# Layer 2's differential attention: a tile's transposes directly behind the next tile's scores, with the filling matmuls after them

## The chip, the cores and the metric

The kernel runs on one core of a Trainium2 chip. The metric is the time of one execution in device microseconds. A core has TensorE (matmuls and transposes into PSUM banks), VectorE, ScalarE, GpSimd and the DMA queues; the engines run side by side and wait for each other through semaphores. In the profile PE is TensorE's matmuls, PEld its weight loads, DVE is VectorE, ACT ScalarE, POOL GpSimd, SP the queue that issues most loads.

## The reference

A two-layer backbone with 512 latent tokens, 256 context tokens, a width of 1024. Each layer has a mixer of four branches (Fourier, convolution, grouped-query attention, differential attention), gated and merged, and then a SwiGLU part. In the second layer only the 512 latent tokens are updated, and they read all 768. The branch that the change touches:

```python
def diff_attend(q, k, v, lam):
    s = jnp.einsum("bhmqd,bhmkd->bhmqk", q, k).astype(jnp.float32) * (DIFF_QK_DIM ** -0.5)
    p = jax.nn.softmax(s, axis=-1)
    w = (p[:, :, 0] - lam * p[:, :, 1]).astype(v.dtype)
    return jnp.einsum("bhqk,bhkd->bhqd", w, v)
```

There are four heads; each has two score maps (m = 0 and 1), and a root-mean-square norm follows on each head's output.

## The kernel before, in words

All large matmuls are done on operands split into a high and a low part, three matmuls for one product (L607 to L609 in the filling units). The differential attention runs through `steps`, four heads by four tiles of 128 queries in layer 2 (`last` is true, `nqt` is 4). For a tile:

- `issue(i)` puts the tile's scores on TensorE (L904, eight matmuls into the one PSUM buffer `pS`) and the negated row maximum on VectorE (L910, L912).
- `exps` makes the two exponentials on ScalarE (L923), which read `pS`.
- `combine` makes the weights of the difference in place in `es[0]` on VectorE (L1379, L1380, L1382).
- `transp` transposes that tile on TensorE (L933, six transposes into two PSUM banks of the tag T, named `pT`), copies them on ScalarE as the high part (L935) and subtracts for the low part on VectorE (L936).
- In every second tile (p odd) 18 matmuls multiply by the values (L1432), two transposes spread the sums (L1437), and L1442 and L1443 write the output.

The work is in a stretch of manual schedule: TensorE, VectorE and ScalarE take instructions in the order in which the program issues them. Between these parts the program issues filling: `fill.run(w)` first pumps side work, then issues chunks of gate units (six matmuls of 512 columns each, some 1.4 us), as far as its budget reaches. In layer 2 the budget of a step is 3.84 us of matmuls, shared out by `DF = (0.55, 0.15, 0.3, 0.0)` over four places in the step. A gate unit has four chunks of a gate's projection, a tanh on ScalarE (L779), two chunks of the branch's product, and VectorE's merge (L786, L787). After each chunk `stream.feed` keeps the weights coming: loads (L557 on SP's queue), the cast of the high part on ScalarE (L563), the low part on VectorE (L570).

Side work is a list of generators, each with the matmul time (`clk`) before which it isn't resumed. `pump` resumes those that are due:

```python
for e in list(self.side):
    if e[1] <= clk[0]:
        next(e[0])
        e[1] = clk[0] + gap
```

Two of them use T banks on TensorE: `od_norm`, the norm of a head's output, parked at the end of its head and resumed in the next (L1218 square, L1226 sums into a bank, L167 and L169, L1234 transposes into a bank, L1235), and `conv_ln`, the convolution's layer norm, in head 0 (L948, L951, L955 mean into a bank, L957 to L963, later L970 and L977). The tag T has two banks:

```python
def bank():
    return pp.tile([P, 512], F32, tag="T", name="pT", bufs=2)
```

The last tile's step of a head (`end`) makes the next head's keys, queries and values in place of the filling.

Of the kernel before, what the change touches and what calls it, by code (L numbers as in the profile page):

```python
# [62 lines left out]
def block_kernel(ctx: ExitStack, tc: tile.TileContext, x, c, ctx_in, c_ctx, w_ada, b_ada, norm_mix, w_in,  # L63
# [148 lines left out]
    def drain(g):  # L212
        for _ in g:
            pass
# [36 lines left out]
    def bank():  # L251
        return pp.tile([P, 512], F32, tag="T", name="pT", bufs=2)
# [366 lines left out]
    for l in range(DEPTH):  # L619
        last = l == DEPTH - 1  # L620
# [5 lines left out]
        GF, DF = GF_[l], DF_[l]  # L626
# [3 lines left out]
        with ExitStack() if l else first as st:  # L630
# [27 lines left out]
            def pttile():  # L658
                t = sp.tile([P, 2, 6, 2 * P], F32R, tag="pt", name="pt", bufs=1)
                return t, t.rearrange("p w k (i q) -> p w k i q", i=2)  # L660
# [43 lines left out]
            def run_taps(n, free=False):  # L704
                with ExitStack() if free else tc.issue_after(lastv[0]):
                    for _ in range(min(n, len(tapq))):
                        tapq.pop(0)()
# [186 lines left out]
            def scores(q, k, ks, t, ko, nk):  # L894
                S = sbank()
                for a in range(2):
                    cuts = [0, 512, NTOK] if a == 0 else [0, 256, NTOK]
                    for c0, c1 in zip(cuts, cuts[1:]):
                        c1 = min(c1, nk)
                        if c0 >= c1:  # L900
                            continue
                        for i in range(2):
                            clk[0] += (c1 - c0) / 2400.0
                            nc.tensor.matmul(S[:, a, c0:c1], lhsT=q[:, a, t * P:(t + 1) * P],  # L904
                                             rhs=k[i][:, ks[a], ko + c0:ko + c1], start=(i == 0), stop=(i == 1))
                return S

            def row_max(S, nk, scale):
                nm = smp.tile([P, 2], F32, tag="nm", name="nm")
                nc.vector.reduce_max(nm, S[:, :, :nk], axis=AX.X, negate=True)  # L910
                if isinstance(scale, float):
                    nc.vector.tensor_scalar(nm, nm, scale, None, op0=ALU.mult)  # L912
                else:
                    nc.vector.tensor_mul(nm, nm, scale)
                return S, nk, scale, nm

            def exps(S, nk, scale, nm):
                ss = smp.tile([P, 2], F32, tag="ss", name="ss")
                es = []
                for a in range(2):  # L920
                    e = etile(nk, "e")
                    sc = scale if isinstance(scale, float) else scale[:, a:a + 1]
                    nc.scalar.activation(e, S[:, a, :nk], AF.Exp, bias=nm[:, a:a + 1], scale=sc, accum_out=ss[:, a:a + 1])  # L923
                    es.append(e)
                return es, ss

            def transp(e, pt, i, nkt):
                clk[0] += nkt * 0.107
                for a in range(0, nkt, 4):
                    b = min(nkt, a + 4)  # L930
                    pb = bank()
                    for t in range(a, b):
                        nc.tensor.transpose(pb[:, (t - a) * P:(t - a + 1) * P], e[:, t * P:(t + 1) * P], ident)  # L933
                    src = pb[:, :(b - a) * P].rearrange("p (t q) -> p t q", q=P)
                    nc.scalar.copy(pt[:, 0, a:b, i], src)  # L935
                    nc.vector.tensor_sub(pt[:, 1, a:b, i], src, pt[:, 0, a:b, i])  # L936

            def krange(t):
                return (0, NTOK) if t < 4 else (X, CT)
# [52 lines left out]
            def conv_split(i0, i1):  # L992
                rr = [(0, X, 0)] if last else [(0, X, 0), (X, NTOK, CO)]
                for i in range(i0, i1):
                    y = stile([2, NTOK], F32R, "yc")
                    for a, b, o in rr:
                        v = ca[i][:, o:o + b - a]
                        nc.scalar.copy(y[:, 0, a:b], v)
                        nc.vector.tensor_sub(y[:, 1, a:b], v, y[:, 0, a:b])
                    yc.append(y)  # L1000

            def ytile(name):
                return sp.tile([P, NT], F32, tag="y", name=name, bufs=4 if last else 2)
# [170 lines left out]
            def wt(t):  # L1174
                return 1.0 if t < 4 else 0.45
# [75 lines left out]
            with tc.manual_schedule(engines=ENG):  # L1251
# [5 lines left out]
                fill = Filler()  # L1257
# [20 lines left out]
                def issue(i):  # L1278
                    j, t = steps[i]
                    ko, nk = krange(t)  # L1280
                    S = scores(qbox[j], qbox["k"], (j // 2, j // 2), t, ko, nk)
                    rq = qs[j][1]
                    return row_max(S, nk, rq[:, 2 * t:2 * t + 2])
# [111 lines left out]
                for i, (hd, t) in enumerate(steps):  # L1395
                    p = i % nqt
                    if cln is None and not tapq:
                        cln = conv_ln()
                        fill.park(cln, 0.0)
                    if hd == 3 and p == nqt - 1:  # L1400
                        drain(cln)
                        conv_split(0, 3)
                    if p == 0:
                        o = ytile("yd")
                        yd.append(o)
                        v = box["v"]
                    ko, nk = krange(t)
                    k0, nkt_ = ko // P, nk // P
                    end = p == nqt - 1
                    if not end:  # L1410
                        nm_ = issue(i + 1)
                        fill.run(wt(t) * DF[0])
                    elif hd < 3:
                        fill.rest()
                        fill.take()
                    if p % 2 == 0:
                        pt, pt5 = pttile()
                    transp(w_, pt5, p % 2, nkt_)
                    if not end:
                        es = exps(*nm_)  # L1420
                        fill.run(wt(t) * DF[1])
                    elif hd < 3:
                        fill.take()
                        dv = fill.take(True)
                    else:
                        fill.rest()
                    if p % 2 == 0:
                        pvs = pp.tile([P, 512], F32, tag="pv", name="pv", bufs=1)
                    if p % 2 == 1:
                        for i_, (vi, pi) in enumerate(((0, 0), (1, 0), (0, 1))):  # L1430
                            for kt in range(nkt_):
                                nc.tensor.matmul(pvs[:, :256], lhsT=v[:, vi, k0 + kt], rhs=pt[:, pi, kt],  # L1432
                                                 start=(kt == 0 and i_ == 0), stop=(kt == nkt_ - 1 and i_ == 2))
                        clk[0] += nkt_ * 0.32
                        lo = (t - 1) * P
                        for u_ in range(2):
                            nc.tensor.transpose(pvs[:, 256 + u_ * P:256 + (u_ + 1) * P],  # L1437
                                                rss[p - 1 + u_][:, 0:1].to_broadcast([P, P]), ident)
                    if not end:
                        fill.run(wt(t) * DF[2])  # L1440
                    if p % 2 == 1:
                        nc.scalar.copy(o[:, lo:lo + 256], pvs[:, :256])  # L1442
                        nc.vector.tensor_mul(o[:, lo:lo + 256], o[:, lo:lo + 256], pvs[:, 256:])  # L1443
                    if not end:
                        w_ = combine(*es, rss)
                        run_taps(NTD[l], True)
                        fill.run(wt(t) * DF[3])
                    else:
                        fill.park(od_norm(o))
                        if hd < 3:  # L1450
                            drain(dv)
                            fill.catch_up()
                            rss = []
                            nm_ = issue(i + 1)
                            fill.g = fill.nx
                            fill.nx = dunits(hd + 2) + gu[2 * hd + 4:2 * hd + 6] if hd < 2 else []
                            fill.b = 0.0
                            fill.run(0.5)
                            es = exps(*nm_)
                            fill.run(0.5)  # L1460
                            w_ = combine(*es, rss)
# [250 lines left out]
```

## Time and profile before

| | |
|---|---|
| median of 3 runs | 2641.51 us (2640.91 to 2641.99) |
| the profiled execution, its own time | 2644.01 us |
| its span | 2642.2 us |
| granted TensorE clock, mean | 0.993 of full |
| TensorE busy | 97% of the span |
| VectorE, ScalarE busy | 65%, 43% |
| stretch of layer 2's differential attention | 1862 to 2080 us |

Times in the rows are microseconds from the span's start, except the mean of one instruction, which is in ns. The span is from the first to the last instruction. A row of the timeline merges equal instructions that follow each other (x is their number): start, busy time, engine, line, operation, out<-in, shapes, and in brackets the idle time of the engine before it with what ended it. Matmuls overlap in the pipeline, so the distance between starts tells more than the busy time of one.

### The profile page before, as it was taken

The page shows a single profiled execution, that of the slowest core. Times are in us where ns is not written, and L with a number is a line of the kernel's source. Part 1 is how long each engine was busy: PE and PEld are TensorE (multiplying, and loading weights), DVE is VectorE, ACT ScalarE, POOL GpSimd, SP SyncE. Part 2 cuts the span into 40 slices and gives each one's busy share as a digit, 9 for nine tenths or more (in the row PEclk, how much of TensorE's full clock was granted, in tenths as well). Part 3 has the DMA queues.
Part 4 walks back from the last instruction along what each step waited for, and adds up shares of the span by engine and source line. Part 5 has one row for each costly group of instructions (what it writes and reads, how often), then busy time and mean ns, then how long its engine had stood idle before and what let it go on. Part 6 is the DMA issues. An engine that isn't in the chain of part 4 may idle for free.

```text
span 2642.2 us, 38743 instructions
## 1 busy us (share of the span) xinstructions
PE 2564.4 (97%) x14651; PEld 2349.2 (89%) x14651; DVE 1710.8 (65%) x3042; ACT 1129.2 (43%) x2262; POOL 113.1 (4%) x179
## 2 busy tenths in 40 slices
PE   7999999999999999999999999999999999999998
PEld 5999889999999989999999988788888888988887
DVE  4967887777778667463353579987766635733335
ACT  5235555455522246212212254566655424623235
POOL 1000000010000000000000000100000000000000
PEclk8999999999999999999999999999999999999999
DMA  8211112222255355343353453111222234533334
GB/s 278 78 45 45 39 39 72 57 54 59 78 153 154 115 162 161 93 128 96 90 158 96 135 147 88 52 41 53 68 80 69 76 96 144 161 100 96 96 95 137
DMA packets 401760, 263.07 MB, mean 100 GB/s; under 512 B 15883, under 2 KB 369493, under 8 KB 401573
## 3 DMA queue, kind: packets, MB, share of 16 engines
q1 hardware_dynamic: 394292, 236.67, 30.3%
q0 software_dynamic: 7280, 23.93, 3.2%
q8 instruction: 115, 1.88, 0.3%
q14 instruction: 73, 0.59, 0.1%
HBM read 243.75 MB, written 8.91 MB: 96 GB/s over the span
## 4 chain that ended last, share of the span: by engine, by line
PE 84%; DVE 5%; ACT 4%; DMA 3%; issue 3%; POOL 0%; DVEq 0%; SPq 0%; POOLq 0%; ACTq 0%
PE pf L525 14%; PE pf L523 14%; PE pf L524 14%; PE pf L607 10%; PE pf L608 10%; PE pf L609 10%; PE pS L904 3%; PE pT L933 2%; PE pv L1343 2%; DMA ws<-in_w_ffn_dram 1%; PE pv L1432 1%; ACT e L923 1%; DVE wl L220 1%; DMA ws<-in_w_out_dram 1%; ACT wh L218 1%
## 5 line engine op out<-in xcount | busy, mean ns | idle before, releaser
L218 ACT CAST wh<-ws 128x512 fp32r<-128x512 f32 (+1 forms) x432 | 261.9, 608 | 582.8 <-PE pf L524 441.7
L523 PE MATMUL pf<-h,wh 128*128 128x384 f32 (+2 forms) x1360 | 468.4, 347 | 3.8 <-ACT tg L728 1.5
L524 PE MATMUL pf<-h,wh 128*128 128x384 f32 (+2 forms) x1360 | 468.4, 346 | 1.1 <-DVE h L181 1.1
L525 PE MATMUL pf<-h,wl 128*128 128x384 f32 (+2 forms) x1360 | 467.9, 346 | 0.5 <-DVE wl L220 0.4
L220 DVE TENSOR_TENSOR wl<-ws,wh 128x512 fp32r<-128x512 f32 (+1 forms) x432 | 289.5, 673 | 267.1 <-ACT wh L218 264.2
L607 PE MATMUL pf<-h,wh 128*128 128x384 f32 (+1 forms) x1280 | 459.1, 359 | 1.9 <-ACT tg L779 1.3
L609 PE MATMUL pf<-h,wl 128*128 128x384 f32 (+1 forms) x1280 | 449.0, 351 | 0.0
L608 PE MATMUL pf<-h,wh 128*128 128x384 f32 (+1 forms) x1280 | 447.8, 350 | 0.0
L523 PEld LDWEIGHTS pf<-h,wh 128*128 128x128 f32 x1360 | 254.9, 188 | 25.0 <-ACT h L180 2.8
L524 PEld LDWEIGHTS pf<-h,wh 128*128 128x128 f32 x1360 | 255.8, 188 | 20.9 <-DVE h L181 2.7
L525 PEld LDWEIGHTS pf<-h,wl 128*128 128x128 f32 x1360 | 255.5, 188 | 20.0 <-DVE wl L220 1.3
L563 ACT CAST wh<-ws 128x512 fp32r<-128x512 f32 x264 | 164.2, 623 | 236.1 <-PE pf L608 198.3
L607 PEld LDWEIGHTS pf<-h,wh 128*128 128x128 f32 x1280 | 241.4, 189 | 16.4 <-ACT tg L779 2.0
L608 PEld LDWEIGHTS pf<-h,wh 128*128 128x128 f32 x1280 | 241.6, 189 | 13.5 <-issue 0.7
L609 PEld LDWEIGHTS pf<-h,wl 128*128 128x128 f32 x1280 | 240.9, 188 | 13.4 <-issue 0.2
L570 DVE TENSOR_TENSOR wl<-ws,wh 128x512 fp32r<-128x512 f32 x264 | 181.1, 687 | 98.2 <-ACT wh L563 96.7
L701 DVE SCALAR_TENSOR_TENSOR ca<-ub,cols,ca 128x798 f32<-128x798 f32 (+1 forms) x240 | 215.3, 897 | 3.9
L525 PE MATMUL pf<-g,wl 128*128 128x384 f32 (+2 forms) x584 | 198.9, 341 | 1.3 <-DVE wl L220 1.1
L523 PE MATMUL pf<-g,wh 128*128 128x384 f32 (+2 forms) x584 | 199.2, 342 | 0.2
L130 DVE SCALAR_TENSOR_TENSOR wada<-wada,sil 128x512 f32<-128x512 f32 x224 | 162.5, 747 | 56.3 <-DMA wada<-in_w_ada_dram 55.0
L524 PE MATMUL pf<-g,wh 128*128 128x384 f32 (+2 forms) x584 | 197.7, 339 | 0.0
L935 ACT CAST pt<-pT 128x512 fp32r<-128x512 f32 (+1 forms) x216 | 91.9, 471 | 154.7 <-PE pT L933 154.2
(324 smaller groups left out, 4068.1 us busy)
## 6 DMA issues: line engine op xcount, KB each, us to landing
ws<-in_w_ffn_dram SPq DMA_DIRECT2D x284, 256.0 KB, 2.9
ws<-in_w_in_dram SPq DMA_DIRECT2D x248, 256.0 KB, 2.9
wada<-in_w_ada_dram SPq DMA_DIRECT2D x160, 256.0 KB, 3.0
ws<-in_w_out_dram SPq DMA_DIRECT2D x58, 256.0 KB, 2.9
ws<-in_w_ffn_dram SPq DMA_DIRECT2D x48, 192.0 KB
wada<-in_w_ada_dram SPq DMA_DIRECT2D x16, 512.0 KB, 6.8
khl<-khl POOLq DMA_DIRECT2D x40, 192.0 KB, 3.2
ws<-in_w_four_dram SPq DMA_DIRECT2D x16, 256.0 KB, 2.8
```

Source lines behind the costliest of these rows:

```text
L130: nc.vector.scalar_tensor_tensor(accs[r], w, s, accs[r], op0=ALU.mult, op1=ALU.add)
L218: nc.scalar.copy(wh[:, :n], st[:, :n])
L220: lastv[0] = nc.vector.tensor_sub(wl[:, :n], st[:, :n], wh[:, :n]).ins
L523: nc.tensor.matmul(o, lhsT=wh, rhs=xh(k), start=(k == 0), stop=False)
L524: nc.tensor.matmul(o, lhsT=wh, rhs=xl(k), start=False, stop=False)
L525: nc.tensor.matmul(o, lhsT=wl, rhs=xh(k), start=False, stop=(k == n - 1))
L563: nc.scalar.copy(wh, u.raw[len(u.wh)])
L570: nc.vector.tensor_sub(wl, u.raw[i], u.wh[i])
L607: nc.tensor.matmul(o, lhsT=wh, rhs=xh(k), start=(k == 0), stop=False)
L608: nc.tensor.matmul(o, lhsT=wh, rhs=xl(k), start=False, stop=False)
L609: nc.tensor.matmul(o, lhsT=wl, rhs=xh(k), start=False, stop=(k == nk - 1))
L701: nc.vector.scalar_tensor_tensor(a, u, w, a, op0=ALU.mult, op1=ALU.add)
```

## The change

In layer 2, in the steps that aren't a head's last, `transp` of the tile is called right after `issue` of the next one, and the filling of DF[0] after `transp`; before, it was the other way round. Layer 1 and the last steps keep their order.

```diff
                     if not end:
                         nm_ = issue(i + 1)
+                    if not end and not last:
                         fill.run(wt(t) * DF[0])
-                    elif hd < 3:
+                    elif end and hd < 3:
                         fill.rest()
                         fill.take()
                     if p % 2 == 0:
                         pt, pt5 = pttile()
                     transp(w_, pt5, p % 2, nkt_)
+                    if not end and last:
+                        fill.run(wt(t) * DF[0])
                     if not end:
                         es = exps(*nm_)
                         fill.run(wt(t) * DF[1])
```

## Rows read from the trace of the kernel before

**Rows 1.** The page, its first part: busy time, share of the span and instructions of each engine.

```profile
PE 2564.4 (97%) x14651; PEld 2349.2 (89%) x14651; DVE 1710.8 (65%) x3042; ACT 1129.2 (43%) x2262; POOL 113.1 (4%) x179
```

**Rows 2.** TensorE's waits from 1862 to 2080 us: the waiting line, what it waited for, total us, times, longest.

```profile
PE pS L904 <- ACT e L923: 4.4, 4, 1.1
...
PE pv L1432 <- ACT pt L935: 1.8, 4, 0.5
```

**Rows 3.** The timeline in head 0, some rows of the steps 0 (from 1868.67), 1 (from 1876.25) and 2 (from 1886.88).

```profile
1868.67 1.67 PE L904 MATMUL pS<-khl,qhl 128*128 128x512 f32 x8
...
1870.17 0.39 PE L607 MATMUL pf<-h,wh 128*128 128x512 f32 x1
...
1870.90 1.02 DVE L1382 SCALAR_TENSOR_TENSOR e<-e,ss 128x768 f32<-128x768 f32 x1
...
1876.25 1.68 PE L904 MATMUL pS<-khl,qhl 128*128 128x512 f32 x8 [1.11 <-ACT e L923]
...
1880.52 0.82 PE L933 MATMUL pT<-ident,e 128*128 128x128 f32 x6
...
1881.79 2.79 PE L1432 MATMUL pv<-pt,vd 128*128 128x256 f32 x18 [0.46 <-ACT pt L935]
...
1884.63 1.02 PE L955 MATMUL pT<-cs,mean 128*128 128x512 f32 x2
...
1886.88 1.56 PE L904 MATMUL pS<-khl,qhl 128*128 128x512 f32 x8
...
1888.29 0.39 PE L607 MATMUL pf<-h,wh 128*128 128x512 f32 x1
...
1889.54 1.02 DVE L1382 SCALAR_TENSOR_TENSOR e<-e,ss 128x768 f32<-128x768 f32 x1
```

**Rows 4.** The timeline of step 0 of head 1, some rows.

```profile
1928.92 1.68 PE L904 MATMUL pS<-khl,qhl 128*128 128x512 f32 x8
...
1929.36 1.02 DVE L1382 SCALAR_TENSOR_TENSOR e<-e,ss 128x768 f32<-128x768 f32 x1
1930.43 0.95 PE L1226 MATMUL pT<-ones,osq 128*128 128x1 f32 x8
1930.63 1.76 DVE L910 TENSOR_REDUCE nm<-pS 128x2 f32<-128x1536 f32 x1 [0.26 <-PE pS L904]
1931.24 0.47 PE L607 MATMUL pf<-h,wh 128*128 128x512 f32 x1
...
1932.50 0.15 DVE L167 TENSOR_SCALAR var<-pT 128x4 f32<-128x4 f32 x1
...
1932.71 0.39 PE L607 MATMUL pf<-ygh,wh 128*128 128x512 f32 x1
...
1932.91 0.60 ACT L779 ACTIVATE tg<-pf 128x512 f32<-128x512 f32 x1 [3.01 <-PE pf L609]
...
1933.40 0.61 ACT L563 CAST wh<-ws 128x512 fp32r<-128x512 f32 x1
1934.09 0.82 PE L933 MATMUL pT<-ident,e 128*128 128x128 f32 x6
1934.66 0.48 PE L607 MATMUL pf<-ygh,wh 128*128 128x512 f32 x1
...
1935.47 0.92 ACT L923 ACTIVATE e<-pS,nm 128x768 f32<-128x768 f32 x1
...
1937.41 1.68 PE L904 MATMUL pS<-khl,qhl 128*128 128x512 f32 x8 [1.11 <-ACT e L923]
```

**Rows 5.** The timeline of step 1 of head 1 and the start of its step 2 (1947.24), some rows.

```profile
1937.85 1.02 DVE L1382 SCALAR_TENSOR_TENSOR e<-e,ss 128x768 f32<-128x768 f32 x1
1938.93 0.60 PE L1234 MATMUL pT<-ident,r 128*128 128x128 f32 x4
...
1939.29 0.48 PE L607 MATMUL pf<-h,wh 128*128 128x512 f32 x1
...
1941.00 0.74 DVE L1235 SCALAR_TENSOR_TENSOR yd<-yd,cols,pT 128x512 f32<-128x512 f32 x1
...
1942.13 0.82 PE L933 MATMUL pT<-ident,e 128*128 128x128 f32 x6
...
1943.41 2.40 PE L1432 MATMUL pv<-pt,vd 128*128 128x256 f32 x18 [0.46 <-ACT pt L935]
...
1947.24 1.56 PE L904 MATMUL pS<-khl,qhl 128*128 128x512 f32 x8
1947.25 1.02 DVE L1382 SCALAR_TENSOR_TENSOR e<-e,ss 128x768 f32<-128x768 f32 x1
...
1948.64 0.40 PE L607 MATMUL pf<-h,wh 128*128 128x512 f32 x1
```

**Rows 6.** The timeline in layer 2's grouped-query attention, where a tile's second transposes follow its first.

```profile
1764.56 1.00 DVE L936 TENSOR_TENSOR pt<-pT,pt 128x512 fp32r<-128x512 f32 x2
...
1765.28 0.87 PE L933 MATMUL pT<-ident,e 128*128 128x128 f32 x6 [1.91 <-DVE pt L936]
```

**Rows 7.** Stretches of the span, TensorE alone: start and end, length, its busy time (instructions), the granted clock as a share of full, the DMA engines' busy share, GB/s. The first two are in layer 1, the third is head 1.

```profile
461.37:464.78 3.41, 1.92 (x9) 1.00 0.19 55
464.78:468.19 3.41, 3.41 (x13) 0.50 0.02 5
1924.00:1980.00 56.00, 54.43 (x309) 1.00 0.27 73
```

## The prediction

> **What bounds the kernel now.** I read the page first. TensorE is busy for 97% of the span [rows 1], so any time it stands still is paid at the end, and a gain must come out of its idle time. The list of TensorE's waits in the stretch of layer 2's differential attention (1862 to 2080 us, four heads) shows what there is to win: scores that wait for the exponentials, 4.4 us in four waits, one per head, and value products that wait for the copy of the transposed weights, 1.8 us in four [rows 2]. The timeline of one whole step, in order, says why [rows 4]. The scores of the next tile are issued at 1928.92. The filling matmuls (L607 to L609) come behind them, and the transposes (L933) only at 1934.09. ScalarE runs in program order and has the two copies of the transposes (L935) ahead of the exponentials (L923), so those start at 1935.47, and the scores after them, which need the one score buffer, can't start before 1937.41. In the step after, the products L1432 follow the transposes with no filling between, and wait for the copy [rows 5].
>
> The budget of filling per step is 3.84 us. By DF it comes out as two chunks of six matmuls at DF[0], none at DF[1], one at DF[2]; the two groups of L607 between 1931.24 and 1934.09 are the two at DF[0], four matmul triples [rows 4].
>
> **The change, part by part.** No instruction is added or dropped. In 12 steps (three of four tiles in each head; the last tile's step stays) the six transposes, their two ScalarE copies and two VectorE subtractions move ahead of DF[0]'s two chunks and of all that these chunks issue: side work pumped, tanh and gate products, weight casts and the weight loads on SP's queue. No load of its own moves past another; SP's weight loads hang on the VectorE subtraction L570, which now comes behind L936, about 1 us later. TensorE has no wait for L570 in the list [rows 2], so I cost that at nothing; if that cover were gone it is some 0.5 us in a step.
>
> What the order removes, by head: the wait of 1.11 for the exponentials (1.3 with the pipeline's restart) and that of 0.46 for the copy [rows 4, 5]. Four heads give some 7.5 us.
>
> What it makes late is new. Three things stand in TensorE's queue now with nothing in front to cover them.
>
> First, the transposes need the combined tile e (L1382). In heads 1 to 3 it ends at 1929.36 + 1.02 = 1930.38 and the scores are through at 1930.43: no wait [rows 4]; in the next steps 1938.87 against 1938.93, and 1948.27 against 1948.64 [rows 5]. Head 0 differs, below.
>
> Second, the banks. Tag T has two, and transp takes both. The pump at DF[0] is the next thing after it, and in heads 1 to 3 it issues od_norm of the head before: L1226 in step 0, L1234 in step 1, each right after the scores in the trace [rows 4, 5], and each takes a T bank. Now it must wait until the first subtraction L936 has freed one. The pump's clock only runs ahead by the transposes' 0.64, so both stay at that pump. VectorE runs in order too, and has the 1.76 us maximum (L910) and L912 ahead of the subtractions. They can start where the next VectorE operation starts now: 1932.50, which is 3.58 after the scores began, and in step 1 1941.00, 3.59 after [rows 4, 5]. The trace has this very wait in the grouped-query part: subtractions from 1764.56, TensorE on again at 1765.28, 0.72 later, after standing 1.91 [rows 6]. So L1226 and L1234 start 4.3 us after the scores began. The transposes take 0.57 (1934.09 to 1934.66) and are over at 2.1 us: TensorE stands 2.2 us, and the filling meant to cover is queued behind the waiting matmul.
>
> Third, ScalarE. In step 0 DF[0]'s chunks finish a gate product, and its tanh (L779) and a cast (L563) come ahead of the exponentials in ScalarE's order [rows 4]. They wait for the chunk, which has moved later.
>
> Step 0 of heads 1 to 3, from the start of the scores: bank at 4.30; L1226 0.81 (1930.43 to 1931.24), 5.11; first chunk 1.47 (1931.24 to 1932.71), 6.58; tanh 0.20 behind it, 6.78; cast 0.49 later, 7.27; exponentials after its 0.61, 7.88; from their start to the next scores 1.94 (1935.47 to 1937.41), 9.82. It is 8.49 now: 1.33 longer, although the old wait is spent [rows 4].
>
> Step 1: bank at 4.31; L1234 0.36, 4.67; two chunks 2.84 (1939.29 to 1942.13), 7.51; products and a chunk without their wait 3.83 (1943.41 to 1947.24), 11.34, against 9.83: 1.5 longer. The exponentials are done by then, since no tanh stands ahead [rows 5]. Step 2 has no side work with a bank: 0. Per head 2.8, three heads 8.5 us.
>
> Head 0 has no od_norm, but its combined tile is late. Step 0: e ends at 1870.90 + 1.02, 3.25 after the scores began, while these are through at 1.5 [rows 3]. With 0.2 to reach TensorE, transposes 0.57, chunk 1.47, tanh 0.20, cast 0.49 + 0.61 and 1.94 the step is 8.73; it is 7.58 now: 1.15 longer. Step 1 wins: the gap of 1.27 between transposes and products shrinks to 0.57, the products take 2.40 as in the other heads for 2.79 [rows 3, 5], together with 0.1 left for the start: 1.0 shorter. Step 2: the convolution's norm (L955) puts its VectorE work ahead of the combine, which ends 1889.54 + 1.02 = 1890.56, 5.93 after L955, while the scores are through after 3.66 (1888.29) [rows 3]. Today two chunks hide that; then TensorE stands 2.5 with the hand-over. Head 0 is 2.65 longer.
>
> The sum: 8.5 + 2.65 = 11 us more than the profiled execution's 2644.0 (span 2642.2), so 2655.0 there, and 2652.5 against the median 2641.5 of the runs, which lies 2.5 under the profiled one.
>
> Bounds: no row shows how long a bank is held here, only one in the other attention. With its idle time of 1.91 for my 2.2, six waits give 1.7 less; if both subtractions must end, some 0.5 each, 3 more. Head 0's 2.5 may be lost in full, or eaten by waits of the head's last step. Together 6 to 14 us; I take 11, since each link is in program order.
>
> The old wait is the same 1.11 in every head. The Trainium skill, "Perfetto Trace Analysis", section "Optimization Strategy", says that a gap which repeats on the engine that should be saturated can mean too little PSUM for the next tile. That speaks against a cure by order alone: by it the 7.5 us would come back at another buffer, a change of 0; my sum has it come back larger, at the T banks. No row here settles it ahead of the run.
>
> **Rivals.**
> *The full gain, no new wait*: 7.5 us go, 2634.0. For it speaks that the maximum hides under the filling today. Against it L1226 and L1234, which the trace puts at that pump in each later head. 0.05.
>
> *No bank wait, the rest as told* (the side matmuls find a free bank, or the subtractions are done before them): heads 1 to 3 have 9.82 - 2.2 against 8.49 and 11.34 - 2.2 against 9.83, 1.6 gained per head, 4.7 in all; head 0 still loses 2.65: 2639.5, no change that could be measured. It decides if TensorE reaches the pump later than 4.3 us after the scores began; by the rows it is there at 2.1. 0.09. With partial cover elsewhere (a few us longer, under 2646.8) another 0.06.
>
> *The clock falls as well.* The granted clock is 1.00, the 2.4 GHz level, in this stage [rows 7], with waits of 1.1 in each head. In layer 1 a stretch in which TensorE was busy 1.92 of 3.41 us is followed by one of 3.41 us at 0.50, the 1.2 GHz level [rows 7]; it did half the work, so 1.7 us are lost. Six new waits of 2.2 us, each among short transposes or one-column matmuls, could bring up to three of these, 5 us: 2657.5. Against it: the new waits are single ones between full-rate matmuls, as today's are. 0.18.
>
> The Trainium skill, "TensorE: Matmul & The Clock Gate", section "Part 4: PE-mode transpose", says that transposes don't count as a busy TensorE for the clock. Moving them beside a wait would then make a fall likelier, and the time that of this last rival; no row here tells transposes from other work in this.
>
> **How the numbers follow.** The forecast (waits for banks and for e, clock as now) has 0.62, the fall of the clock 0.18, no bank wait 0.09, partial cover 0.06, full gain 0.05. 0.2% is 5.3 us, about what a measurement of this kernel can tell from no change. Slower is then 0.62 + 0.18 = 0.80, same 0.09 + 0.06 = 0.15, faster 0.05. The forecast's own range is 2647.5 to 2655.5; taking in the clock, 2646.5 to 2658.
>
> **What would show it.** In the profile after: L904's waits for L923 shrink from 1.1 to 0.5 or less, and L1432 has none for L935; L1226 and L1234 wait for L936, six times, about 2.2 us each, longest in the list; L933 waits for L1382 twice, in head 0, 1.9 and 2.5 us; heads 1 and 2 grow by 2.8 us each. I am wrong if L1226 and L1234 don't wait, or if step 0's exponentials start before its tanh.

## The result and the profile after

The changed kernel takes 2661.1 us (median of four, 2655.4 to 2665.8) against 2641.2 (the kernel before with a fourth run; the prediction's sum starts from 2641.5): a ratio of 1.0076 with an interval of 1.0063 to 1.0089, 20 us slower. Slower was forecast, but by 11 us, and the range ended at 2658.

The profiled execution is the shortest of the four, 2655.38 us with a span of 2653.5. The two spans can't simply be subtracted: up to the stage both run the same program, yet the changed kernel reached it 5 us earlier. So the stage is measured by itself, from head 0's first scores to the first matmul that reads the convolution's output (L607 pf<-yc). In the timeline of the changed kernel these are:

```profile
1858.01 1.64 PE L904 MATMUL pS<-khl,qhl 128*128 128x512 f32 x8
...
2082.97 0.50 PE L607 MATMUL pf<-yc,wh 128*128 128x512 f32 x1 [0.37 <-ACT tg L779]
```

The stage and what lies behind it as stretches, TensorE alone (start and end, length, busy time and instructions, granted clock, DMA share, GB/s), in the kernel before:

```profile
1862.99:2071.97 208.98, 199.93 (x1107) 1.00 0.24 66
2071.97:2642.20 570.23, 556.30 (x2964) 0.99 0.39 114
```

and in the changed one:

```profile
1858.01:2082.97 224.96, 206.86 (x1108) 0.97 0.22 62
2082.97:2653.50 570.53, 556.05 (x2964) 0.99 0.39 114
```

The stage grew by 16.0 us, and behind it nothing changed (570.5, and 570.2 before). Two things are new in it. TensorE is busy only for 207 of 225 us, 18 us idle after 9 before; and its mean granted clock, 1.00 before, is 0.97.

The list of TensorE's waits in the stage (1862 to 2092 us) answers [rows 2]:

```profile
PE pT L1234 <- DVE pt L936: 6.0, 3, 2.1
PE pT L1226 <- DVE pt L936: 5.8, 3, 1.9
PE pT L933 <- DVE e L1382: 3.9, 2, 2.3
...
PE pS L904 <- ACT e L923: 0.4, 2, 0.2
```

The old waits are gone, 4.4 for the exponentials down to 0.4 and those for the copy altogether. In their place stand six waits for a T bank and two for the combined tile: 15.7 us. The timeline of step 0 of head 1 shows the bank's chain, and answers [rows 4]:

```profile
1925.52 1.66 PE L904 MATMUL pS<-khl,qhl 128*128 128x512 f32 x8
...
1927.03 0.87 PE L933 MATMUL pT<-ident,e 128*128 128x128 f32 x6
1927.22 1.76 DVE L910 TENSOR_REDUCE nm<-pS 128x2 f32<-128x1536 f32 x1 [0.24 <-PE pS L904]
...
1929.01 0.17 DVE L912 TENSOR_SCALAR nm<-nm 128x2 f32<-128x2 f32 x1
1929.09 1.01 DVE L936 TENSOR_TENSOR pt<-pT,pt 128x512 fp32r<-128x512 f32 x2
...
1929.83 1.05 PE L1226 MATMUL pT<-ones,osq 128*128 128x1 f32 x8 [1.92 <-DVE pt L936]
...
1930.74 0.48 PE L607 MATMUL pf<-h,wh 128*128 128x512 f32 x1
...
1932.41 0.60 ACT L779 ACTIVATE tg<-pf 128x512 f32<-128x512 f32 x1 [3.83 <-PE pf L609]
...
1932.91 0.61 ACT L563 CAST wh<-ws 128x512 fp32r<-128x512 f32 x1
...
1933.41 0.91 ACT L923 ACTIVATE e<-pS,nm 128x768 f32<-128x768 f32 x1
...
1935.35 1.66 PE L904 MATMUL pS<-khl,qhl 128*128 128x512 f32 x8 [0.17 <-ACT e L923]
```

L1226 gets its bank 4.31 us after the scores began (forecast: 4.30), the exponentials start behind tanh and cast, and the step takes 9.83 (forecast: 9.82; before: 8.49).

The granted clock tells the rest. These are the four falls in the stage, each with the stretch ahead of it (columns as above):

```profile
1936.50:1939.92 3.42, 1.46 (x11) 1.00 0.01 2
1939.92:1943.33 3.41, 3.41 (x11) 0.50 0.00 0
...
1987.70:1991.12 3.42, 1.50 (x14) 1.00 0.00 0
1991.12:1994.53 3.41, 3.41 (x10) 0.50 0.25 73
2049.15:2052.56 3.41, 2.07 (x13) 1.00 0.00 0
2052.56:2055.97 3.41, 3.41 (x10) 0.50 0.26 77
2059.39:2062.80 3.41, 1.33 (x9) 1.00 0.26 77
2062.80:2066.21 3.41, 3.41 (x10) 0.50 0.00 0
```

Each fall to 0.50, the 1.2 GHz level, comes right behind a stretch in which TensorE was busy for 1.3 to 2.1 us, with a wait for L936, or the end of one, in it. The two other bank waits stood in stretches as little busy (1926.27 and 1997.95), and the clock stayed at full behind them:

```profile
1926.27:1929.68 3.41, 1.64 (x12) 1.00 0.04 10
1929.68:1933.09 3.41, 3.26 (x18) 1.00 0.03 10
1997.95:2001.36 3.41, 1.63 (x12) 1.00 0.09 27
2001.36:2004.77 3.41, 3.23 (x16) 1.00 0.02 5
```

So a wait with little work around it stood ahead of every fall here, but it did not bring one each time, and why it was these four of the six is not shown.

What one fall costs can be read from the same step in different heads:

```profile
1948.34 1.56 PE L904 MATMUL pS<-khl,qhl 128*128 128x512 f32 x8
...
1997.13 1.67 PE L904 MATMUL pS<-khl,qhl 128*128 128x512 f32 x8
...
2008.56 1.56 PE L904 MATMUL pS<-khl,qhl 128*128 128x512 f32 x8
```

Step 1 of head 2 has its wait but no fall, and takes 11.43 us (1997.13 to 2008.56); step 1 of head 1 has a fall in it and takes 12.99 (1935.35 to 1948.34). That is 1.56 for this fall; the three others cost 1.22 to 1.42 by the same comparison. The four falls make 5.5 us. Without them steps 0 and 1 are 1.3 and 1.6 us longer than before in each of three heads, and head 0 is 1.6 longer: 10.4 us. Both together are the 16.0 by which the stage grew.

### The profile page after: what moved, and what is told of

It is laid out like the page before. It is cut to its first block, busy times and chain, and to the rows that moved or that the text cites. A ratio compares the mean times of both kernels' runs of the same rounds, so it can differ in the third digit from the quotient of the medians.

```text
span 2653.5 us, 38747 instructions
## 1 busy us (share of the span) xinstructions
PE 2567.5 (97%) x14651; PEld 2351.7 (89%) x14651; DVE 1712.5 (65%) x3042; ACT 1130.3 (43%) x2262; POOL 113.3 (4%) x179
## 4 chain that ended last, share of the span: by engine, by line
PE 84%; DVE 6%; ACT 4%; issue 3%; DMA 3%; POOL 0%; DVEq 0%; POOLq 0%; SPq 0%; ACTq 0%
PE pf L525 14%; PE pf L524 14%; PE pf L523 14%; PE pf L607 10%; PE pf L608 10%; PE pf L609 10%; PE pS L904 3%; PE pT L933 2%; PE pv L1343 2%; DMA ws<-in_w_ffn_dram 1%; PE pv L1435 1%; DVE nm L910 1%; ACT e L923 1%; DVE pt L936 1%; DVE wl L220 0%
## 5 line engine op out<-in xcount | busy, mean ns | idle before, releaser
L607 PE MATMUL pf<-h,wh 128*128 128x384 f32 (+1 forms) x1280 | 461.8, 361 | 1.4 <-ACT tg L779 1.4
L607 PEld LDWEIGHTS pf<-h,wh 128*128 128x128 f32 x1280 | 242.7, 190 | 15.5 <-ACT tg L779 2.0
```

The lines of the kernel that those rows point to most:

```text
L607: nc.tensor.matmul(o, lhsT=wh, rhs=xh(k), start=(k == 0), stop=False)
```

## Experiments

The kernel before was timed again beside the first four runs, with a median of 2641.5 us, and beside the last four, with 2639.6. So ratios are compared, and in the last four a time expected against 2641.5 has to be read 2 us lower. Lines of the kernels are moved by a few against the kernel before.

**The change again** (no edit).

> The changed kernel once more, to see how its time spreads. Theory A (six waits for a T bank and two for the combined tile make 11 us, and what is above that is TensorE's granted clock falling behind these waits, 1.6 us a fall): 2655 to 2666 us again, with 4 to 8 stretches of half clock in layer 2's differential attention, and the time of a run following its mean granted clock. Rival B (the excess over 11 us has another cause, such as weights that come late): times as far apart as before, but not in step with the clock.

2660.4 us, ratio 1.0067 (1.0054 to 1.0079). The same eight waits, and five falls in the stage, one of them in head 0. The stage took 226.5 us, 1.5 more than with four falls. The other four falls stand in the same steps as in the first profile: step 1 of head 1, step 0 of head 2, steps 0 and 1 of head 3. Theory A holds in the stage.

The profiled stages grew by 16 and 17.5 us; the medians by 20 and 19, and both profiled executions are the shortest of theirs. Mean clocks of whole executions bear on the difference, as far as their three digits go: the nine executions of the changed kernel have 0.988 to 0.992, those of the kernel before 0.992 to 0.995. An estimate from their averages, 0.9897 of the nine and 0.9937 of the sixteen beside this run: the 0.004 between them are 10.6 us of clock, or some 6 falls of 3.41 us at half clock, which at 1.2 to 1.6 us each make 18 to 20 us with the 10.4 of the waits. That the other executions have a fall or two more in the stage fits this, but no trace of them shows it. A mean clock also holds the falls outside the stage, of which every profile has some.

**The pump behind the chunks.** What waits for the bank is moved, not the wait taken away.

```diff
-                def run(self, w):
-                    self.pump()
+                def run(self, w, pump=True):
+                    if pump:
+                        self.pump()
...
                     if not end and last:
-                        fill.run(wt(t) * DF[0])
+                        fill.run(wt(t) * DF[0], False)
```

> The change, but in layer 2 the side work isn't pumped at DF[0], so that the norm of the last head asks for a T bank only behind two filling chunks. Theory A: the six waits of L1226 and L1234 for L936 are gone and the half clock behind them too; heads 1 to 3 gain some 2 us each against the kernel before; head 0 keeps its wait for the combined tile in step 0 (1.8 us), and perhaps that in step 2, each perhaps with a fall of the clock: 2637 to 2643 us in all. Rival C (the time freed comes back as a wait at another buffer): 2648 us or more, with a new wait of 1 us or more per step in the list.

2641.3 us, ratio 1.000 (0.999 to 1.001), inside theory A's range. All six bank waits and the falls behind them are gone, and heads 1 to 3 took 54.0, 54.0 and 34.9 us for 56.0, 56.0 and 36.8 before. Head 0 ate most of this up: 64.7 for 60.3. From the list of TensorE's waits in the stage:

```profile
PE pT L933 <- DVE ca L980: 2.2, 1, 2.2
PE pT L933 <- DVE e L1383: 1.6, 1, 1.6
PE pT L970 <- DVE vs L963: 1.2, 1, 1.2
```

The wait for the combined tile in step 0 stayed, that of step 2 was gone, as the convolution's norm had moved into the head's last step, and there it made two new ones and the stage's one fall. The longer of the two, 2.2 us, is a wait for a T bank again, as the timeline of this last step shows: four transposes go through, and the other two wait until L980 (ca<-ca,pT) has read the norm's bank.

```profile
1899.50 0.60 PE L933 MATMUL pT<-ident,e 128*128 128x128 f32 x4
1902.33 0.41 PE L933 MATMUL pT<-ident,e 128*128 128x128 f32 x2 [2.23 <-DVE ca L980]
```

So what rival C says came about in head 0 and not in the others; its number, 2648 us, was missed.

**Heads 1 to 3 alone.** The edit before, and head 0 in the old order:

```diff
+                    new = last and hd > 0
-                    if not end and not last:
+                    if not end and not new:
                         fill.run(wt(t) * DF[0])
...
-                    if not end and last:
+                    if not end and new:
                         fill.run(wt(t) * DF[0], False)
```

> As the run before, with head 0 in the old order. Theory A: no wait for a bank, none for the combined tile: 6 us under the kernel before, 2635 us. Rival C: no better than the kernel before, 2641 us or more.

2634.75 us, ratio 0.9971 (0.9959 to 0.9982): 7 us faster than the kernel before, and as theory A put it. The stage took 203.1 us with no fall, 5.8 less than before, 1.9 to 2.0 in each of three heads. The timeline of step 0 of head 1:

```profile
1924.80 1.68 PE L904 MATMUL pS<-khl,qhl 128*128 128x512 f32 x8
...
1926.31 0.87 PE L933 MATMUL pT<-ident,e 128*128 128x128 f32 x6
1926.51 1.76 DVE L910 TENSOR_REDUCE nm<-pS 128x2 f32<-128x1536 f32 x1 [0.26 <-PE pS L904]
...
1926.94 0.48 PE L607 MATMUL pf<-h,wh 128*128 128x512 f32 x1
...
1928.38 1.02 DVE L936 TENSOR_TENSOR pt<-pT,pt 128x512 fp32r<-128x512 f32 x2
...
1929.60 0.91 ACT L923 ACTIVATE e<-pS,nm 128x768 f32<-128x768 f32 x1
1929.79 0.94 PE L1227 MATMUL pT<-ones,osq 128*128 128x1 f32 x8
...
1932.08 1.55 PE L904 MATMUL pS<-khl,qhl 128*128 128x512 f32 x8
```

The subtractions are as late as in the changed kernel, but while VectorE works on the maximum TensorE has the two chunks. L1227 (the old L1226) finds its bank free, and the exponentials are through by the time TensorE is. The step takes 7.28 us where it took 8.49.

**Matmuls in the waits.** Nine matmuls whose result is not used stand in each of the six waits:

```diff
                     if not end and last:
+                        if p == 0:
+                            pvs = pp.tile([P, 512], F32, tag="pv", name="pv", bufs=1)
+                        if hd > 0 and p < 2:
+                            for _ in range(9):
+                                nc.tensor.matmul(pvs, lhsT=h[:, 0, 0, 0:P], rhs=h[:, 0, 0, 0:512], start=True, stop=True)
                         fill.run(wt(t) * DF[0])
...
-                    if p % 2 == 0:
+                    if p % 2 == 0 and (p or not last):
                         pvs = pp.tile([P, 512], F32, tag="pv", name="pv", bufs=1)
```

> The change, with nine matmuls of 512 columns whose result is not used, put on TensorE between the transposes and the pump in steps 0 and 1 of heads 1 to 3 (2.05 us, as long as the wait for the bank). It computes the same as the changed kernel. Theory A: TensorE loses the same 11 us, but is busy meanwhile, so the half clock behind the six waits is gone: 2651 to 2656 us, up to two falls in head 0 included. Rival B: the clock isn't what makes the excess, 2660 us as the changed kernel.

2654.8 us, ratio 1.0044 (1.0031 to 1.0056), inside theory A's range and 6 us under the changed kernel on the same chip, with 54 matmuls more. L1226 starts where it did, as the timeline of step 0 of head 1 shows:

```profile
1925.81 1.66 PE L904 MATMUL pS<-khl,qhl 128*128 128x512 f32 x8
1927.32 0.88 PE L933 MATMUL pT<-ident,e 128*128 128x128 f32 x6
1927.95 2.33 PE L1425 MATMUL pv<-h 128*128 128x512 f32 x9
1930.12 1.05 PE L1226 MATMUL pT<-ones,osq 128*128 128x1 f32 x8
```

It is again 4.31 us after the scores, so the delay is the same; yet heads 1 to 3 had no fall, and their steps 0 and 1 took 9.8 and 11.4 to 11.7 us. The one fall left was in head 0, whose two waits weren't filled. This separates the two costs in the stage: the late bank costs the same whether TensorE stands or works, and what the stage lost beyond that was the clock. Rival B, which put this run at 2660 us, is refuted.

**The maximum behind the subtractions.** In layer 2 `issue` leaves out `row_max`, and it is called behind `transp`:

```diff
                     if not end and last:
+                        nm_ = row_max(*nm_, 0.125)
                         fill.run(wt(t) * DF[0])
```

> The change, with the row maximum of the next tile behind the two subtractions in VectorE's order. Theory A (the bank is held for so long because the maximum, 1.76 us, stands ahead of the subtraction): the six waits for L936 shrink from 2.0 to 1.1 to 1.4 us, about 5 us in all, and fewer of them are followed by half clock; head 0 pays up to 1 us in step 0 because its exponentials come later: 2650 to 2657 us. Rival D (the bank waits for ScalarE's copy or for TensorE itself, not for the maximum): waits of 2.0 us as in the change, 2660 us.

2650.6 us, ratio 1.0036 (1.0021 to 1.0050). The six waits were 3.8 and 3.5 us in all, 1.2 each for 2.0, and two falls were left in the stage, each behind a wait of L1226. The list of TensorE's waits:

```profile
PE pT L933 <- DVE e L1382: 4.2, 3, 2.3
PE pT L1234 <- DVE pt L936: 3.8, 3, 1.3
PE pT L1226 <- DVE pt L936: 3.5, 3, 1.2
...
PE pS L904 <- ACT e L923: 1.4, 2, 1.2
```

So the maximum's place in VectorE's order makes some 0.75 us of each wait, and rival D is refuted for that part. The other 1.2 are transposes, copy and subtraction by themselves: the subtraction now waits for ScalarE's copy (1.36 us in step 0 of head 1). Head 0's exponentials came later, as expected (L904, 1.2).

**One chunk ahead, one behind,** in the old order:

```diff
-DF_ = ((0.4, 0.25, 0.2, 0.15), (0.55, 0.15, 0.3, 0.0))
+DF_ = ((0.4, 0.25, 0.2, 0.15), (0.2, 0.5, 0.3, 0.0))
```

> The order of the kernel before, but with layer 2's filling shared out as 0.2, 0.5, 0.3, 0, so that one chunk stands between scores and transposes and one behind the transposes. Theory A: the wait for the exponentials (1.1) goes in all heads, a chunk covers most of the waits for the bank and the combined tile (0.6 us left in step 1, 0.5 and 1.1 in head 0): 2636 to 2640 us. Rival E (any shift of the transposes ahead of filling pays as much in new waits as it saves): 2641 us or more.

2641.1 us, ratio 1.0007 (0.9999 to 1.0016): no gain, and theory A's number missed. Step 0 got shorter as expected (7.59 for 8.49), but step 1 got longer (10.1 to 10.4 for 9.8) and step 2 with the head's last tile too (32.4 to 32.5 for 32.0), so that heads 1 and 2 gained only 0.1 to 0.2 us each; head 0 lost 1.2. The last head is 1.8 us longer for another reason: it holds a dozen matmuls more, and what lies behind the stage has ten fewer and is 1.9 us shorter. The time is the one that rival E gave, though the run with heads 1 to 3 alone refutes it for shifts of every kind. The list of TensorE's waits has new ones:

```profile
PE pv L1432 <- DVE pt L936: 4.5, 4, 1.2
...
PE pf L607 <- ACT tg L779: 1.7, 4, 1.1
```

With one chunk less ahead, the products catch up with the subtractions, which still stand behind the maximum: 1.1 us per head, which I had put at 0.6.

**Head 0 alone** in the changed order (`new = last and hd == 0`, otherwise the kernel before).

> The change in head 0 alone, the other heads in the order of the kernel before. Theory A: two waits for the combined tile (1.6 and 2.3 us), two old waits gone: 1.6 to 2.7 us longer, and up to two falls of the clock of 1.6 us: 2643 to 2647 us. If head 0 weren't a loss by itself it would be 2641 us or less.

2642.5 us, ratio 1.0011 (1.0002 to 1.0020), some 3 us longer than the 2639.6 beside it, as theory A put it once its range is read against that time. The profiled stage grew by 1.6 us with no fall in it; head 0 is a loss by itself.

**Head 0's filling split,** on the kernel of heads 1 to 3 alone (DF 0.2, 0.5, 0.3, 0 in head 0):

> The kernel of e2 (heads 1 to 3 in the new order with the pump behind the chunks, head 0 in the old order), with head 0's filling shared out as 0.2, 0.5, 0.3, 0. Theory A: 0 to 1.5 us under e2, 2633 to 2635 us; a rival in which head 0's late combined tile costs more than the split saves: 2635 to 2637 us.

2636.0 us, ratio 0.9985 (0.9975 to 0.9994); its profiled stage took 204.4 us for 203.1 without the split. Head 0 lost 1.2 us by the split, so the rival was right about its sign. The version with heads 1 to 3 alone has the lowest ratio, though the two intervals overlap.

## Why the prediction was right or wrong

The direction was right, and so were the places and causes of all eight waits. By its steps:

- *What goes*: right. The waits for the exponentials went from 4.4 us to 0.4, those for the copy to nothing.
- *The bank in heads 1 to 3*: right. Step 0 was put at 9.82 and took 9.83, step 1 at 11.34 and took 11.43 where the clock stood; three heads make 8.8 for the 8.5 forecast. With a fall in each, heads 1 and 2 grew by 4.5 and 4.3 and not by the 2.8 that were to show it. That VectorE's order makes part of the wait, 0.75 of 2.0 us, was tested by the run with the maximum behind.
- *Head 0*: right in kind, too large. It lost 1.6 us for my 2.65. Both waits for the combined tile came (1.6 and 2.3 us), but step 2 with the head's last tile grew by 1.5 and not by 2.5: the old wait of 0.6 for the copy L1183 in the last tile went. I had named this as a bound and hadn't taken it.
- *The clock*: wrong, and this is the step that put the time outside the range. Four and five falls in the two profiled stages, none before. I gave them a rival's 0.18 and at most three, and argued against them that the new waits were single ones between full-rate matmuls, as today's. They aren't: the old ones (1.1 us) stood between filling and scores, the new ones (2.0) have six transposes ahead and one-column matmuls or more transposes behind, and TensorE was busy for only 1.3 to 2.1 us of the 3.41 ahead of each fall behind them. The rows that make this likelier than 0.18 were there: [rows 7] show a fall behind a stretch that was busy 1.92 of 3.41, and my own step times put 2.2 us of idle time into each of six places. No row could tell which waits bring a fall, but four of six, at the 1.7 of the estimate, would have added 6.8 us to the sum: 2659.3. The falls in the traced stages make 5.5 and some 7 us; the 2 to 4 us by which the medians grew more than these stages stay open but for the estimate from the mean clocks.
- *The price of a fall* was 1.7 by the estimate, 1.2 to 1.6 in the runs.
- *Two sums* beside the forecast don't come out: 1.3 and 0.46 in four heads make 7.0 us and not 7.5, and the bounds as named lead from 6.9 us and not from 6. The 11 us hold neither.

The two rules of the Trainium skill: that a repeating gap can mean too little PSUM ("Perfetto Trace Analysis", section "Optimization Strategy") is half borne out. The time did come back at another buffer, the T banks. But no bank was added in the run with heads 1 to 3 alone, and there the order by itself gave 5.8 us in the stage. That transposes don't count as a busy TensorE for the clock ("TensorE: Matmul & The Clock Gate", section "Part 4: PE-mode transpose") was not tested: that run has the same transposes in the same place and no fall, but no wait beside them either.

## What to carry to other kernels

When work is moved ahead of its filling, look for the next instruction that wants the same buffer, not only at the operands of what is moved: here that was side work of another head, and the whole engine queued behind it. Moving that one request behind the filling too took away the loss of 20 us, and with head 0 left in the old order there was a gain of 7. And price a new wait on TensorE with the clock: look how little work is left around it, since a fall cost 1.2 to 1.6 us where the wait itself was 2.0.

## What the runs showed of the hardware

A wait of 2 us, and in two cases one of 1.2, was enough to take the clock to 1.2 GHz for 3.41 us when short transposes and one-column matmuls stood beside it: eight falls behind the twelve bank waits of the two profiled stages, two behind the six waits of 1.2 us in the run with the maximum behind, none with the same delay filled by matmuls.

The busy time by itself doesn't tell which wait brings a fall: the clock fell behind a stretch with 2.07 us of work and stayed at full behind two with 1.64 and 1.63. In both profiles of the changed kernel it was the same four of the six bank waits, while a fall in head 0 came in one of them only. The nine executions of the changed kernel span 10 us; that falls make this difference is not shown.
